# Where sequence 1's attention operands are made: inside layer 0's second MLP product, or behind it

## The chip, the cores and the metric

The kernel runs on one core of one Trainium2 chip. The metric is the device time of one execution in microseconds. The kernel before takes 1729.86 us (median of 3 runs, 1728.86 to 1730.07).

The core has a matrix engine (TensorE, "PE" in the profile, with its weight loads as "PEld"), a vector engine (VectorE, "DVE"), an activation engine (ScalarE, "ACT"), a general engine (GpSimd, "POOL"), and a sync engine (SyncE, "SP") that here only issues transfers. Each engine works off its own queue of instructions in a fixed order; an instruction that waits holds up everything behind it on its engine. Matmuls write to PSUM, eight banks of 128 x 512 floats. Everything else lies in SBUF.

## What is computed

Two sequences (512 tokens, 1024 features each, float32) go through two layers and a final norm:

```
x = x + fourier_mix(rms_norm(x, fourier_norm))            # layer 0
x = x + sq_relu_mlp(rms_norm(x, mlp_norm[0]))
x = x + gqa_attention(rms_norm(x, attn_norm), ...)        # layer 1
x = x + sq_relu_mlp(rms_norm(x, mlp_norm[1]))
y = rms_norm(x, final_norm)
```

with

```
rms_norm(x, g)   = x * rsqrt(mean(x*x, features) + 1e-6) * g
sq_relu_mlp(h)   = (max(h @ w_up, 0) ** 2) @ w_down       # 1024 -> 4096 -> 1024
gqa_attention(h) : qkv = h @ w_qkv (1024 -> 1536); q and k each rms_norm'ed per head of 128
                   and rotated; 8 query heads on 2 key/value heads; softmax; @ w_o
```

The change lies at the seam between layer 0's MLP and layer 1's attention.

## The kernel before

**Precision.** Every float32 matrix is split into a high half, which the matmul reads in its fast float32r form, and a low half, the rest. A product is then three matmuls: high by high, high by low, low by high (`mm3`, L76, and `product`, L827). A split is one ACT cast (L82, or with a gain per feature L86) and one DVE subtraction (L83, or L87).

**Layout.** The residual is kept with features on the partitions: `xs[q, m]` is a tile of 128 x 2 x 512 (feature blocks 2m and 2m+1, 512 tokens) for sequence q and m from 0 to 3. Most work tiles come from four pools: `u4` with 38 slots of 4 KB per partition (`slot()`, L61), `t2` with 8 of 2 KB (`tm()`, L64), `raw` with 5 for weights as they are loaded, and `w` with 4 for split weights (`own()`).

**The second MLP product of layer 0** (`second_product`, L1061, called at L1366) multiplies the 4096 hidden features of both sequences by `w_down`. It uses a block scheme of Winograd's kind: for each output pair m it keeps a shared sum `e[m]` and adds partial products to both sequences' `xs[q, m]`. Its steps are `Row` (two products of 12 matmuls) and `Sums` (five products of 12: t1, t3, t2, b22, t4), over four groups g of hidden features. The last group's four `Sums` (m = 0 to 3) close the product. For each, DVE forms sums of the raw weights (L1147 to L1149, L1155), splits them (L83), and adds the PSUM results to the residual (L1080). When all steps of m are done, `finish(m)` (L1241) adds `e[m]` to sequence 0 (L1244) and to sequence 1 (L1245), and calls `ready(m)`.

**What ready(m) does.** For both sequences it makes the two attention operands `hT[q][2m]`, `hT[q][2m+1]` (`make_h`, L177: ACT L86 and DVE L87, 128 x 512 each, with attn_norm as the gain), squares the two feature blocks on ACT (L157), adds the squares to `acc[q]` on POOL (L159; the first of a sequence needs no addition), and stores `xs[q, m]` to DRAM (`put_away`, L186, an SP transfer). The last of these closes the use of `xs[q, m]`, one `u4` slot.

**What follows.** PE starts attention with `begun` (L1482): the key/value columns (cg = 2) of sequence 0's four token tiles t, feature blocks 0 to 5, 18 matmuls each. Then comes `token_scale(0)` (L1349): `sums` (L161, eight tiny matmuls of `acc[0]` by ones, line L165) and a chain of small DVE and ACT instructions (L131 to L137) that gives the root r = rsqrt(mean square) of every token. Then, tile by tile, the last two feature blocks are added (6 matmuls), and the result is evacuated with the factor r: ACT L1507 for keys, ACT L86 and DVE L87 (128 x 256) for values, then the norm of the keys and the rotation (`norm_rope`, L1398, ending in the POOL addition L1423 into `kr[q]`). After tile 0's six matmuls stands `token_scale(1)`. Sequence 1's four tiles follow, 24 matmuls each. Before tile 2 of sequence 1, PE transposes sequence 0's keys (`transpose_k`, L1429, matmul line L1433), for which all four tiles of `kr[0]` must be there. In the same stretch DVE makes the rotation tables (L1378, 16 small instructions) and splits the next `w_qkv` weights (L83).

**What sets the order.** Inside `tc.manual_schedule(engines=...)` the named engines keep the order of the Python code. In the product's main loop (L1309) that is PE alone. For all other engines there, and for all engines from the end of the product up to the last stage's hand-ordered blocks, a planner in the framework makes one fixed order per engine before the run: it plays the program through and gives each engine the ready instruction that comes first in the code. A tile takes a slot of its pool when the planner places the first instruction that writes it. The functions that the change touches, and their callers:

Of the kernel before, what the change touches and what calls it, by code (L numbers as in the profile page):

```python
# [21 lines left out]
NSEQ = 2  # L22
NT = S // P
KC = D // P
# [16 lines left out]
def trunk_kernel(ctx, tc, x_in, xt_in, y_out, dcos, dsin, feat, rope, gfour, gcol, grow, gfin,  # L41
# [15 lines left out]
    def nm(s):  # L57
        n_[0] += 1
        return f"{s}_{n_[0]}"

    def slot(shape, dt):  # L61
        return act.tile(shape, dt, tag="u4", name=nm("u"))

    def tm(shape=(P, 512), dt=F32):  # L64
        return tmp.tile(list(shape), dt, tag="t2", name=nm("t"))
# [19 lines left out]
    def split_scaled(dst_hi, dst_lo, src, scale):  # L85
        nc.scalar.activation(dst_hi, src, AF.Copy, scale=scale)  # L86
        nc.vector.scalar_tensor_tensor(dst_lo, src, scale, f32(dst_hi), ALU.mult, ALU.subtract)  # L87
# [22 lines left out]
    def load_w(src, eng=nc.vector, parts=1, home=own):  # L110
        raw = load_raw(src)
        w = home()
        for i in range(parts):
            sl = slice(i * 1024 // parts, (i + 1) * 1024 // parts)
            split(w[0][:, sl], w[1][:, sl], raw[:, sl], eng)
        return w
# [5 lines left out]
    def rsqrt(out, ss, n, inv, room=None):  # L122
        for step in rsqrt_steps(out, ss, n, inv, room=room):
            step()
# [24 lines left out]
    def xt(q, fo):  # L149
        return xs[q, fo // 2][:, fo % 2]  # L150

    def square(q, fo, n=512):

        if fo == 0:
            acc[q] = tm()
        s = tm() if fo else acc[q]
        nc.scalar.activation(s[:, :n], xt(q, fo)[:, :n], AF.Square)  # L157
        if fo:
            nc.gpsimd.tensor_add(acc[q][:, :n], acc[q][:, :n], s[:, :n])  # L159

    def sums(q, n=NT):  # L161

        o = ps()
        for t in range(n):
            nc.tensor.matmul(o[:, 2 * t : 2 * t + 2], acc[q][:, t * P : (t + 1) * P], ones,  # L165
                             start=True, stop=True)
        return o[:, 0 : 2 * n : 2], o[:, 64:]
# [9 lines left out]
    def make_h(q, fo, g0):  # L177

        h = slot([P, 2, 512], F32R)
        split_scaled(h[:, 0], h[:, 1], xt(q, fo), gc[:, g0 + fo : g0 + fo + 1])  # L180
        return h
# [3 lines left out]
    def put_away(q, i):  # L185
        nc.sync.dma_start(park[q, i], xs[q, i])  # L186
# [1160 lines left out]
    hT, rs, wkv = [[], []], [], []  # L1347

    def token_scale(q):  # L1349
        r = sm.tile([P, NT], F32, tag="rs", name=nm("rs"), bufs=2)  # L1350
        ss, room = sums(q)
        rsqrt(r, ss, NT, 1.0 / D, room)
        rs.append(r)
# [2 lines left out]
        for _ in range(2):  # L1356
            wkv.append(load_w(w_qkv[2, len(wkv)], home=lent))

    def ready(m):
        for q in range(NSEQ):  # L1360
            for fo in range(2 * m, 2 * m + 2):
                hT[q].append(make_h(q, fo, KC))
                square(q, fo)
            put_away(q, m)

    second_product(0, blocks, rows, late, ready)  # L1366

    gb = tm((P, 4, HD))
    nc.sync.dma_start(gb, grow.to_broadcast([P, 4, HD]))
# [114 lines left out]
    for cg in (2, 0, 1):  # L1484
        ws = wkv if cg == 2 else [load_w(w_qkv[cg, u], home=own if u < 2 else lent) for u in range(4)]
        for q in range(NSEQ):
            if cg == 2:
                vt[q] = (slot([P, NT, 256], F32R), slot([P, NT, 256], F32R))
                kr[q] = slot([P, NT, 256], F32)
            else:  # L1490
                for i in range(2):
                    qr[q, 2 * cg + i] = slot([P, NT, 256], F32)
            for t in range(NT if (cg, q) != (1, 1) else 2):
                if (cg, q, t) in transposes:
                    transpose_k(transposes[cg, q, t])
                if (cg, q, t) == (1, 1, 1):
                    first = transpose_q(0, 0)
                if (cg, q) == (2, 0):
                    o = qkv(cg, q, t, ws, KC - 2, KC, begun[t])
                else:  # L1500
                    o = qkv(cg, q, t, ws)
                if (cg, q, t) == (2, 0, 0):
                    token_scale(1)
                r = rs[q][:, t : t + 1]
                if cg == 2:
                    raw = tm((P, 256))
                    nc.scalar.activation(raw, o[:, :256], AF.Copy, scale=r)  # L1507
                    split_scaled(vt[q][0][:, t], vt[q][1][:, t], o[:, 256:], r)
                    todo = norm_rope(raw, NKV, rt["k"], [t], [kr[q][:, t]])
                else:  # L1510
                    raw = tm()
                    nc.scalar.activation(raw, o, AF.Copy, scale=r)
                    todo = norm_rope(raw, 4, rt["q"], [t], [qr[q, 2 * cg + i][:, t] for i in range(2)])
                for _ in todo:
                    pass
# [325 lines left out]
```

## Time and profile before

| | |
|---|---|
| timed runs | 1728.86, 1729.86, 1730.07 us |
| the profiled execution's own time | 1727.7 us |
| its span, first to last instruction | 1725.9 us |
| PE busy in the span | 1693.2 us (98%) |
| DVE busy | 1244.9 us (72%) |
| ACT busy | 857.0 us (50%) |
| POOL busy | 332.6 us (19%) |
| PE's first attention matmul | 729.26 us |

The profile shows one execution. Times in it count from the start of its span. A row of the timeline reads: start, duration, engine, line of the kernel, operation, tiles written and read with their shapes, count, and in brackets how long the engine had been idle before it and what ended that. An engine with a "q" behind it is its queue, issuing a transfer. A row with a count above 1 is a run of equal instructions. A row of the windows view gives, for each stretch, each engine's busy time and instruction count, the mean granted TensorE clock (1.00 is full), and the mean share of the transfer engines; an instruction that laps into a stretch from before is counted in it.

### The profile page before, as it was taken

The numbers are of one execution on the slowest core, as the hardware profiler recorded it, in microseconds if no ns is written. First come the engines' busy times: TensorE is split into PE (matmuls) and PEld (weight loads), VectorE is DVE, ScalarE is ACT, GpSimd is POOL, SyncE is SP. The second block draws the span as 40 slices with busy tenths as digits, with TensorE's granted clock in tenths as the row PEclk, the third lists the DMA queues.
The fourth block names the chain that finished last, engine by engine and source line by source line (L and its number), as shares of the span: only waits on it lengthen the run. The fifth ranks groups of instructions, "written<-read, shape, count | busy, mean of one in ns | idle before, by whom it ended". The sixth has DMA issues, their size and how long they took to land. (4 is left out here: it accounts for less than half of the span.)

```text
span 1725.9 us, 21899 instructions
## 1 busy us (share of the span) xinstructions
PE 1693.2 (98%) x7847; PEld 1397.1 (81%) x7847; DVE 1244.9 (72%) x1836; ACT 857.0 (50%) x1508; POOL 332.6 (19%) x302
## 2 busy tenths in 40 slices
PE   9999999999999999999999999999999999999997
PEld 6987777888788888788877888788788888888886
DVE  8678777456887879975588834687755479687865
ACT  6665445446343434456687715554444554344334
POOL 1321442221000001322234303114322200000004
PEclk9999999999999999999999999999999999999999
DMA  9742555449554645520000213335543597455322
GB/s 321 188 153 86 183 183 172 170 172 358 208 195 135 211 147 179 186 88 27 25 25 1 98 49 122 105 123 182 180 150 141 210 305 253 150 211 190 120 74 98
DMA packets 103679, 266.33 MB, mean 154 GB/s; under 512 B 10177, under 2 KB 10177, under 8 KB 103570
## 3 DMA queue, kind: packets, MB, share of 16 engines
q1 hardware_dynamic: 87410, 232.95, 39.0%
q10 hardware_dynamic: 14112, 25.70, 4.0%
q0 software_dynamic: 2048, 6.29, 1.8%
q8 instruction: 61, 1.00, 0.2%
q14 instruction: 48, 0.39, 0.1%
HBM read 189.93 MB, written 73.92 MB: 153 GB/s over the span
## 5 line engine op out<-in xcount | busy, mean ns | idle before, releaser
L833 PE MATMUL ps<-u,w 128*128 128x512 f32 x4704 | 1079.2, 390 | 7.2 <-DVE w L83 5.1
L833 PEld LDWEIGHTS ps<-u,w 128*128 128x128 f32 x4704 | 882.9, 188 | 195.4 <-DVE w L83 7.5
L82 ACT CAST w<-raw 128x1024 fp32r<-128x1024 f32 (+1 forms) x226 | 220.7, 981 | 450.5 <-PE ps L833 260.6
L83 DVE TENSOR_TENSOR w<-raw,w 128x1024 fp32r<-128x1024 f32 (+1 forms) x226 | 263.5, 1168 | 73.9 <-ACT w L82 73.5
L159 POOL TENSOR_TENSOR t<-t,t 128x512 f32<-128x512 f32 (+1 forms) x56 | 80.1, 1434 | 733.1 <-ACT t L157 677.4
L83 DVE TENSOR_TENSOR u<-u,u 128x1024 fp32r<-128x1024 f32 x132 | 157.6, 1220 | 26.7 <-ACT u L82 25.9
L82 ACT CAST u<-u 128x1024 fp32r<-128x1024 f32 x132 | 132.4, 1044 | 71.1 <-PE ps L833 47.5
L77 PE MATMUL ps<-u,u 128*128 128x512 f32 (+2 forms) x388 | 150.1, 388 | 1.9 <-DVE u L496 1.4
L78 PE MATMUL ps<-u,u 128*128 128x512 f32 (+2 forms) x388 | 144.8, 373 | 1.1 <-DVE u L83 1.1
L1080 DVE TENSOR_TENSOR u<-ps,u 128x512 f32<-128x512 f32 x160 | 109.4, 686 | 50.3 <-PE ps L833 49.5
L79 PE MATMUL ps<-u,u 128*128 128x512 f32 (+2 forms) x388 | 144.5, 372 | 0.0
L833 PE MATMUL ps<-u,u 128*128 128x512 f32 x528 | 129.3, 396 | 8.5 <-DVE t L917 8.4
L833 PEld LDWEIGHTS ps<-u,u 128*128 128x128 f32 x528 | 99.0, 190 | 34.6 <-issue 8.0
L941 POOL TENSOR_TENSOR u<-u 128x512 f32<-128x512 f32 x28 | 36.5, 1304 | 422.2 <-ACT u L849 422.2
L83 DVE TENSOR_TENSOR u<-ps,u 128x512 fp32r<-128x512 f32 (+4 forms) x118 | 74.7, 651 | 18.1 <-ACT u L82 16.9
L77 PEld LDWEIGHTS ps<-u,u 128*128 128x128 f32 x388 | 73.5, 189 | 13.5 <-DVE u L496 1.6
L78 PEld LDWEIGHTS ps<-u,u 128*128 128x128 f32 x388 | 73.4, 189 | 13.2 <-DVE u L83 3.0
L79 PEld LDWEIGHTS ps<-u,u 128*128 128x128 f32 x388 | 73.1, 189 | 12.6
L82 ACT CAST u<-ps 128x512 fp32r<-128x512 f32 (+4 forms) x118 | 64.5, 561 | 28.9 <-PE ps L79 11.1
L816 DVE TENSOR_TENSOR u<-ps,u 128x512 f32<-128x512 f32 (+1 forms) x48 | 30.9, 645 | 64.7 <-PE ps L79 64.7
L906 DVE TENSOR_TENSOR t<-ps,u 128x512 f32<-128x512 f32 x30 | 20.7, 690 | 69.2 <-PE ps L833 64.0
L77 PE MATMUL ps<-u,w 128*128 128x512 f32 (+2 forms) x192 | 65.0, 339 | 0.0
(237 smaller groups left out, 1998.3 us busy)
## 6 DMA issues: line engine op xcount, KB each, us to landing
raw<-w_up SPq DMA_DIRECT2D x82, 512.0 KB, 4.6
u<-spill_t SPq DMA_DIRECT2D x60, 512.0 KB, 6.1
raw<-w_sum SPq DMA_DIRECT2D x56, 512.0 KB, 4.0
u<-spill_b SPq DMA_DIRECT2D x45, 512.0 KB, 5.4
spill_t<-u SPq DMA_DIRECT2D x87, 256.0 KB, 2.0
spill_b<-t ACTq DMA_DIRECT2D x60, 256.0 KB, 2.5
raw<-w_row SPq DMA_DIRECT2D x28, 512.0 KB, 4.4
park<-u SPq DMA_DIRECT2D x24, 512.0 KB, 3.0
```

Of the source, the lines that this page charges most:

```text
L77: nc.tensor.matmul(out, lh, rh, start=first, stop=False)
L78: nc.tensor.matmul(out, lh, rl, start=False, stop=False)
L79: nc.tensor.matmul(out, ll, rh, start=False, stop=last)
L82: nc.scalar.copy(dst_hi, src)
L83: eng.tensor_sub(dst_lo, src, f32(dst_hi))
L159: nc.gpsimd.tensor_add(acc[q][:, :n], acc[q][:, :n], s[:, :n])
L816: nc.vector.tensor_add(x[:, :n], o[:, :n], x[:, :n])
L833: nc.tensor.matmul(o, w[x][:, sl], h[k][y], start=first and k + i == 0, stop=k == n - 1 and i == 2, skip_group_check=not first)
L906: nc.vector.tensor_add(u2, ob, t[:, 0])
L941: eng.tensor_sub(t[:, 0], b12, b11)
L1080: nc.vector.tensor_add(x, o, x)
```

## The change

`ready(m)` now takes the sequence as a second argument, 0 if it isn't given. Inside the product it serves sequence 0 alone. Sequence 1's m = 0, 1 and 2 are called in one go behind the product, ahead of the rotation tables and of `begun` and `token_scale(0)` in the code. Sequence 1's m = 3 is called in the first pass of the key/value loop, behind sequence 0's tile 0, and `token_scale(1)` moves from there to behind sequence 1's own tile 0. No computation is added or removed.

```diff
-    def ready(m):
-        for q in range(NSEQ):
-            for fo in range(2 * m, 2 * m + 2):
-                hT[q].append(make_h(q, fo, KC))
-                square(q, fo)
-            put_away(q, m)
+    def ready(m, q=0):
+        for fo in range(2 * m, 2 * m + 2):
+            hT[q].append(make_h(q, fo, KC))
+            square(q, fo)
+        put_away(q, m)
 
     second_product(0, blocks, rows, late, ready)
+    for m in range(3):
+        ready(m, 1)
 
     gb = tm((P, 4, HD))
     nc.sync.dma_start(gb, grow.to_broadcast([P, 4, HD]))
...
                 else:
                     o = qkv(cg, q, t, ws)
                 if (cg, q, t) == (2, 0, 0):
+                    ready(3, 1)
+                if (cg, q, t) == (2, 1, 0):
                     token_scale(1)
                 r = rs[q][:, t : t + 1]
                 if cg == 2:
```

## The prediction

> **What bounds the kernel now.** I read the page first, then PE's waits, then windows around the longest wait, then each engine's timeline there.
>
> ```profile
> span 1725.9 us, 21899 instructions
> PE 1693.2 (98%) x7847; PEld 1397.1 (81%) x7847; DVE 1244.9 (72%) x1836; ACT 857.0 (50%) x1508; POOL 332.6 (19%) x302
> ```
>
> PE is busy for 98% of the span, so the change can only win back time that PE loses, and only where it waits for something that the change touches. PE's waits between 680 and 800 us, the seam:
>
> ```profile
> PE ps L833 <- DVE w L83: 3.9, 2, 2.3
> PE ps L1433 <- POOL u L1423: 0.7, 1, 0.7
> ```
>
> Two waits for split weights (3.9 us) and one for sequence 0's rotated keys (0.7 us). The windows show that the first two cost more than their idle time:
>
> ```profile
> 696.49:709.86 13.37, 13.37 (x60) 11.08 (x59) 13.36 (x16) 9.07 (x13) 6.09 (x4) 1.00 0.25 94
> 709.86:720.87 11.01, 7.12 (x23) 5.13 (x22) 11.01 (x12) 4.82 (x8) 4.18 (x4) 0.85 0.87 296
> 717.15:720.31 3.16, 3.15 (x7) 2.48 (x8) 3.16 (x4) 3.16 (x6) 2.87 (x2) 0.50 1.00 373
> ```
>
> The columns are busy time and count of PE, PEld, DVE, ACT, POOL, then granted clock and transfer share. In the first stretch 59 matmuls start (one lapped in) in 13.37 us: 0.2266 us each. In the second, 22 start; at that pace they need 4.99 us, not 11.01. So PE loses 6.0 us: 3.9 idle, 1.6 in the seven matmuls of the third row at clock 0.50 (3.16 - 7 x 0.2266), and 0.5 in the two restarts. DVE is busy without a break in both stretches: it is the bound there. PE's and DVE's timelines:
>
> ```profile
> 711.83 3.02 PE L833 MATMUL ps<-u,w 128*128 128x512 f32 x12 [1.57 <-DVE w L83]
> 717.16 12.27 PE L833 MATMUL ps<-u,w 128*128 128x512 f32 x46 [2.31 <-DVE w L83]
> 729.26 0.39 PE L77 MATMUL ps<-u,u 128*128 128x512 f32 x1
> ```
> ```profile
> 699.63 0.74 DVE L87 SCALAR_TENSOR_TENSOR u<-u,gc,u 128x512 fp32r<-128x512 f32 x1
> 700.29 1.78 DVE L1149 TENSOR_TENSOR raw<-raw,raw 128x512 f32<-128x512 f32 x1
> 701.99 3.49 DVE L87 SCALAR_TENSOR_TENSOR u<-u,gc,u 128x512 fp32r<-128x512 f32 x2
> 705.40 0.68 DVE L1080 TENSOR_TENSOR u<-ps,u 128x512 f32<-128x512 f32 x1
> 709.47 2.30 DVE L83 TENSOR_TENSOR w<-raw,w 128x1024 fp32r<-128x1024 f32 x1
> 711.70 0.68 DVE L1080 TENSOR_TENSOR u<-ps,u 128x512 f32<-128x512 f32 x1
> 714.03 0.68 DVE L1080 TENSOR_TENSOR u<-ps,u 128x512 f32<-128x512 f32 x1
> 715.29 0.68 DVE L1244 TENSOR_TENSOR u<-u,t 128x512 f32<-128x512 f32 x1
> 715.89 1.21 DVE L83 TENSOR_TENSOR w<-raw,w 128x1024 fp32r<-128x1024 f32 x1
> ```
>
> PE's first wait ends with the L83 of 709.47 (ends 711.77), its second with that of 715.89 (ends 717.10): the splits for the last Sums. Of the three operands made from 699.63 on, the code's order gives sequence 0 the first and sequence 1 the two at 701.99. They hold DVE from 701.99 to 705.40.
>
> **Does the planner really take them out of there?** ACT, POOL and DVE aren't ordered by hand here, and sequence 1's m = 1 is ready as early as before. The trace says that slots are handed out in the order of the code:
>
> ```profile
> 675.90 0.33 SPq L91 DMA_DIRECT2D raw<-w_qkv  x1
> ```
> ```profile
> 698.54 0.72 ACT L86 ACTIVATE u<-u,gc 128x512 fp32r<-128x512 f32 x1 [3.93 <-DVE u L1244]
> 701.44 0.61 ACT L157 ACTIVATE t<-u 128x512 f32<-128x512 f32 x1
> 701.96 1.04 ACT L82 CAST u<-raw 128x1024 fp32r<-128x1024 f32 x1
> 768.61 0.58 ACT L82 CAST u<-ps 128x512 fp32r<-128x512 f32 x1
> ```
> ```profile
> 765.48 0.44 PE L1433 MATMUL ps<-ident,u 128*128 128x128 f32 x2 [0.69 <-POOL u L1423]
> ```
> ```profile
> 768.49 0.74 POOL L1423 TENSOR_TENSOR u<-t,t 128x256 f32<-128x256 f32 x1 [3.06 <-DVE t L1421]
> ```
>
> The first w_qkv weight, sent for at 675.90, is cast at 701.96, although ACT sat idle for 3.93 us before 698.54: directly after ready(1), which stands ahead of it in the code. Sequence 0's transposed keys (the cast at 768.61, ready when the transposes of 765.48 ended) are cast directly behind the first L1423 of kr[1], whose slot was asked for earlier. So sequence 1's operands, now behind sequence 0's m = 3 in the code, can't get slots before it: they do move behind the product. By the same rule hT[1][6] and [7] come after kr[0], that is, after sequence 0's tile 0 has been rotated.
>
> **Step 1, the product's end.** Out of DVE's queue go 705.40 - 701.99 = 3.41 us. The first split then ends at 711.77 - 3.41 = 708.4; PE wants it at 711.83 - 1.57 = 710.26: no wait, 1.9 us in hand. The second ends at 717.10 - 3.41 = 713.7, after the L1080 now at 714.03 (then 710.62; its product ends at 710.26, so it can move that far). PE wants it one product later, at 710.26 + 12 x 0.2266 = 712.98: 0.7 us of wait remain, about 0.1 for its restart. Gain 6.0 - 0.8 = 5.2 us. Upper bound 6.0: with sequence 1's additions gone from POOL beside it, the L1149 of 1.78 us could lose up to 1 us, as an L87 takes 0.74 in one row above and 1.7 in another. Lower bound 3.6, if the half clock, which stands where the transfer share is 1.00, doesn't come from the waits.
>
> The Trainium skill bears on that last point ("TensorE: Matmul & The Clock Gate", Part 1: The HAM clock gate): half rate follows an idle window of about 3.4 us. Here it stands behind 2.31 us of idle, so by the page the 1.6 us wouldn't be the wait's and the gain would be 3.6 us. I take the trace's order of events, wait and then half clock.
>
> ACT's casts and SP's loads of the next weights only come earlier. Of sequence 1's four park transfers three move behind the product, ahead of the tables' input in SP's queue, and one behind tile 0; each holds SP for 0.33 us (as the issue at 675.90), which nobody waits for here.
>
> **Step 2, DVE behind the product.** The rows of before:
>
> ```profile
> 733.62 1.23 DVE L83 TENSOR_TENSOR w<-raw,w 128x1024 fp32r<-128x1024 f32 x1 [1.40 <-ACT w L82]
> 734.77 4.15 DVE L87 SCALAR_TENSOR_TENSOR u<-u,gc,u 128x512 fp32r<-128x512 f32 x3
> 738.84 2.30 DVE L83 TENSOR_TENSOR w<-raw,w 128x1024 fp32r<-128x1024 f32 x1
> 741.06 3.31 DVE L1378 SCALAR_TENSOR_TENSOR u<-raw,t 128x128 f32<-128x128 f32 x16
> 746.57 0.16 DVE L131 TENSOR_SCALAR s<-ps 128x4 f32<-128x4 f32 x1 [2.20 <-PE ps L165]
> ```
> ```profile
> L87 DVE SCALAR_TENSOR_TENSOR u<-u,gc,u x16: 734/744/1784, 668.0 to 737.1; 128x512 fp32r<-128x512 f32 x16
> L159 POOL TENSOR_TENSOR t<-t,t x56: 730/1292/2284, 66.5 to 1705.7; 128x512 f32<-128x512 f32 x49, 128x256 f32<-128x256 f32 x7
> 734.88 5.18 POOL L159 TENSOR_TENSOR t<-t,t 128x512 f32<-128x512 f32 x3 [10.32 <-ACT t L157]
> ```
>
> Sequence 0's root (L131) starts 746.57 - 729.26 = 17.3 us after the product; everything that DVE has ahead of it must fit in that. One L87 takes 0.74 us alone and up to 1.78 beside POOL's additions, which the moved squares bring along (five). I take the row of three with additions beside them, 4.15/3 = 1.38: six make 8.3 us. With the last L1080 and L1244 (1.4), sequence 0's own last L87 (0.7), two L83 (1.2 + 2.3, less 0.7, since only one of them needs to meet an addition, and perhaps not for its whole length) and L1378 (3.3): 16.5 us, and some 0.7 of waiting for ACT: 17.2. It just fits. Bounds: six at 0.74, 4.4 us, leave 4 us spare; six at 1.78, 10.7 us, make the root 2.5 us late. ACT needs 6 x (0.72 + 0.61) = 8 us for them, and POOL five of 1.7 (5.18/3), 8.6 us: both fit.
>
> **Step 3, sequence 1's first block.** In the times of before (everything shifts together):
>
> ```profile
> 762.99 0.70 ACT L1412 ACTIVATE t<-t,s 128x128 f32<-128x128 f32 x2 [1.02 <-DVE s L137]
> 745.59 0.95 PE L165 MATMUL ps<-ones,t 128*128 128x2 f32 x8
> 763.75 0.82 PE L1433 MATMUL ps<-ident,u 128*128 128x128 f32 x6
> 753.59 0.74 POOL L1423 TENSOR_TENSOR u<-t,t 128x256 f32<-128x256 f32 x1 [13.53 <-PE ps L79]
> 757.31 0.73 POOL L1423 TENSOR_TENSOR u<-t,t 128x256 f32<-128x256 f32 x1 [2.98 <-DVE t L1421]
> 764.70 0.72 POOL L1423 TENSOR_TENSOR u<-t,t 128x256 f32<-128x256 f32 x1 [2.99 <-DVE t L1421]
> ```
>
> Tile 0's L1423, now at 753.59, loses the second root from its way: seven small instructions of about 0.16 us (the L131 above), of which I take half to lie in its way, so an estimate of 0.6 us, and 753.0. Then ACT makes hT[1][6], its square, hT[1][7] (0.72 + 0.61 + 0.72, with tile 1's small work between: till 755.6) and DVE the last L87 (up to 1.78, till 757.4). PE comes to these blocks after 0.8 (sums) + 24 + 18 matmuls: 745.59 + 0.8 + 9.5 = 755.9, and needs the last of them at 757.1: 0.3 us of wait. POOL's last addition (1.7 each) ends near 758.2; the sums behind the block want it at 757.6: 0.6. Together +0.8; bounds 0, where the L87 and the additions take 0.74 and 1.29, and 2.5 more, where the root is late.
>
> **Step 4, the key transposes.** They wait 0.69 for tile 3's L1423. That comes 0.6 earlier by the removed root, 0.6 later by the same root in its new place, and later by what ACT's four inserted instructions (2.7 us) exceed its idle time in a tile (1.02 in the L1412 row, some 0.5 more at other waits, an estimate): 1.2. PE arrives 0.8 later: 0.4 more wait. Bounds: -0.7 (the wait is gone) to +2.
>
> **Sum.** -5.2 + 0.8 + 0.4 = -4.0 us. The profiled execution took 1727.7 us (1.8 beside its span), 2.2 under the median of the timed runs: 1723.7 there, 1725.9 as a median.
>
> **Rivals.**
> - *The second split stays late.* Without the two L87 the planner puts other ready work, say a split of w_qkv, in front of it: one L83 of 1.2 to 2.3 us brings its wait back to 2 or more, with the half clock. Only the first wait goes, 1.7 us with its restart: 1729.86 - 1.7 + 1.2 = 1729.4. For it: DVE has no idle time in 13.36 of 13.37 and 11.01 of 11.01 us. Against: 3.41 us go from directly ahead of it.
> - *Sequence 0's root comes late.* L87 and POOL additions in one batch take turns, all at 1.78: root, tile 0, hT[1][6..7] and tile 3 come 2.5 us later. PE pays once, at the first block: -4.0 + 2.5, 1728.4. The Trainium skill gives such a rule ("SBUF — State Buffer", Who interferes with whom): a VectorE instruction with two SBUF inputs and a GpSimd instruction that reads SBUF exclude each other, the later one blocked until the first ends. The 1784 against 734 ns above agrees with blocking.
> - *Slower: hT[1][6..7] come two tiles late.* They must follow kr[0]; if the planner also puts their ACT work behind tiles 1 and 2, L1423's spacing of 3.7 us makes PE's wait at the first block 0.8 + 7.4 = 8.2, with the half clock 9.8, less the transposes' 0.7: 1729.86 - 5.2 + 9.1 = 1733.8. It turns from gain to loss at about one tile. Against: they stand ahead of tile 0's evacuation in the code, so are taken first once slots are there.
> - *It doesn't do what it says.* The planner fills idle ACT and DVE time with sequence 1's work where it is now: 1729.9. Against: the slot order above.
>
> **How the numbers follow.** A measurement of this kernel tells about 0.2% (3.5 us) from no change, so faster means below 1726.4, slower above 1733.3. Chances: forecast 0.49 (0.42 under 1726.4, 0.07 above), second split 0.14 (same 0.12, faster 0.01, slower 0.01), root 0.14 (faster 0.02, same 0.11, slower 0.01), two tiles 0.15 (slower 0.12, same 0.03), no move 0.08 (same 0.06, slower 0.02). That makes 0.45, 0.39, 0.16. The forecast's own range goes from 1729.86 - 6.0 - 0.7 = 1723.2 to 1727.5 (half clock stays). The whole range reaches down to 1722.6 for the scatter of runs, and up to 1731.6, past all cases but two tiles late.
>
> **What would show it.** Right: no PE wait for L83 near 710 and no stretch at clock 0.50; PE's first L77 near 724; behind it six L87 in a row, some at 1.7; the root's L131 within a microsecond after its sums; small waits at the first L165 of acc[1] and at L1433. Wrong: L87 of sequence 1 still among the last Sums; a wait for L83 of 2 us; a wait for L87 of several us at sequence 1's first block.

## The result and the profile after

The changed kernel takes 1735.49 us (median of 6 runs, 1733.89 to 1737.65), the kernel before beside it 1727.81 us (6 runs, 1725.56 to 1730.07). The ratio is 1.0034, with a 95% interval of 1.0019 to 1.0048: slower by 0.0034 x 1728 = 5.9 us (3.3 to 8.3). (The two medians stand 7.7 us apart, inside that interval; the differences in this document go by the ratio.) The forecast was 4.0 us faster. The profiled execution took 1734.09 us, 1.8 of it beside the span.

The head of the page of the changed kernel, span and busy times:

```profile
span 1732.3 us, 21901 instructions
PE 1696.5 (98%) x7847; PEld 1398.9 (81%) x7847; DVE 1246.3 (72%) x1836; ACT 857.4 (49%) x1508; POOL 330.9 (19%) x302
```

The work is the same (PE's and DVE's counts did not move). PE's busy time is up by 3.3 us although it does the same 7847 matmuls: some of them ran slower. PE's waits in the seam, from 640 to 820 us:

```profile
PE ps L1434 <- POOL u L1424: 6.3, 2, 3.2
PE ps L833 <- DVE u L1080: 1.7, 2, 1.4
```

The two waits for the late splits (L83, 3.9 us) are gone. In their place PE waits 1.7 us for L1080 inside the product, and at sequence 0's key transposes, where it had waited 0.7 us, it now waits 6.3 (L1434 and L1424 are L1433 and L1423 of before, one line further down). PE's timeline at the transposes, and the window behind them:

```profile
761.54 0.38 PE L1434 MATMUL ps<-ident,u 128*128 128x128 f32 x2
765.14 0.55 PE L1434 MATMUL ps<-ident,u 128*128 128x128 f32 x3 [3.22 <-POOL u L1424]
768.78 0.90 PE L1434 MATMUL ps<-ident,u 128*128 128x128 f32 x3 [3.09 <-POOL u L1424]
```
```profile
769.00:773.60 4.60, 4.60 (x13) 3.73 (x13) 2.53 (x11) 3.34 (x15) 0.08 (x1) 0.50 0.00 0
```

PE is there two tiles ahead of the keys, and behind the second wait it runs at a granted clock of 0.50 for 4.6 us.

To see where the time went I set the matmuls of both traces side by side in their order and took the difference of their starts at three places. From the first matmul after 690 us to the product's end (the first L77, at 729.26 before and 726.99 after) the changed kernel gains 3.7 us; from there to 780 us it loses 8.2; in the rest it loses another 0.5. The first figure isn't simply 729.26 - 726.99 = 2.3, because the changed kernel's profiled execution was 1.4 us later from the first 100 us on, in code that is the same in both. So the seam costs 4.5 us in the profile. Both parts are what this document explains.

**Where the root went.** DVE's timeline behind the product, and PE's sums for sequence 0's root:

```profile
727.10 1.22 DVE L1245 TENSOR_TENSOR u<-u,t 128x1024 f32<-128x1024 f32 x1
729.02 1.23 DVE L83 TENSOR_TENSOR w<-raw,w 128x1024 fp32r<-128x1024 f32 x1 [0.69 <-ACT w L82]
730.16 0.68 DVE L1080 TENSOR_TENSOR u<-ps,u 128x512 f32<-128x512 f32 x1
730.88 0.69 DVE L1244 TENSOR_TENSOR u<-u,t 128x512 f32<-128x512 f32 x1
732.05 1.23 DVE L83 TENSOR_TENSOR w<-raw,w 128x1024 fp32r<-128x1024 f32 x1 [0.47 <-ACT w L82]
733.19 10.96 DVE L87 SCALAR_TENSOR_TENSOR u<-u,gc,u 128x512 fp32r<-128x512 f32 x7
744.08 5.49 DVE L1379 SCALAR_TENSOR_TENSOR u<-raw,t 128x128 f32<-128x128 f32 x16
749.49 1.41 DVE L87 SCALAR_TENSOR_TENSOR u<-u,gc,u 128x512 fp32r<-128x512 f32 x2
750.81 0.15 DVE L131 TENSOR_SCALAR s<-ps 128x4 f32<-128x4 f32 x1
```
```profile
743.31 0.95 PE L165 MATMUL ps<-ones,t 128*128 128x2 f32 x8
```

The sums end at 743.31 + 0.95 = 744.26 and the root (L131) starts at 750.81: 6.55 us late, with DVE busy throughout. In the kernel before it started 0.03 us after its sums. From 744.08 on DVE works on things that the root doesn't need: the tables and hT[1][6..7]. POOL's timeline beside it:

```profile
736.99 9.81 POOL L159 TENSOR_TENSOR t<-t,t 128x512 f32<-128x512 f32 x6 [0.19 <-POOL t L159]
768.00 0.72 POOL L1424 TENSOR_TENSOR u<-t,t 128x256 f32<-128x256 f32 x1 [2.92 <-DVE t L1422]
```

The tables take 5.49 us beside additions that end at 736.99 + 9.81 = 746.80; two additions lie beside them, and before, with none, the same sixteen instructions took 3.31. And the last rotated key tile comes at 768.00, 17.2 us after the root: tile follows tile at 3.7 us, so a late root is a late last tile.

### The profile page after: what moved, and what is told of

Its sections match the earlier page's. It is cut to its first block, busy times and chain, and to the rows that moved or that the text cites. A ratio compares the mean times of both kernels' runs of the same rounds, so it can differ in the third digit from the quotient of the medians.

```text
span 1732.3 us, 21901 instructions
## 1 busy us (share of the span) xinstructions
PE 1696.5 (98%) x7847; PEld 1398.9 (81%) x7847; DVE 1246.3 (72%) x1836; ACT 857.4 (49%) x1508; POOL 330.9 (19%) x302
## 3 DMA queue, kind: packets, MB, share of 16 engines
q1 hardware_dynamic: 87410, 232.95, 38.8%
## 5 line engine op out<-in xcount | busy, mean ns | idle before, releaser
L83 DVE TENSOR_TENSOR w<-raw,w 128x1024 fp32r<-128x1024 f32 (+1 forms) x226 | 260.1, 1153 | 75.1 <-ACT w L82 74.4
L83 DVE TENSOR_TENSOR u<-u,u 128x1024 fp32r<-128x1024 f32 x132 | 157.8, 1223 | 28.3 <-ACT u L82 27.7
L77 PE MATMUL ps<-u,u 128*128 128x512 f32 (+2 forms) x388 | 151.6, 392 | 1.9 <-DVE u L496 1.4
L1080 DVE TENSOR_TENSOR u<-ps,u 128x512 f32<-128x512 f32 x160 | 109.8, 688 | 51.0 <-PE ps L833 50.3
L833 PEld LDWEIGHTS ps<-u,u 128*128 128x128 f32 x528 | 99.1, 190 | 34.8 <-issue 8.4
L83 DVE TENSOR_TENSOR u<-ps,u 128x512 fp32r<-128x512 f32 (+4 forms) x118 | 74.7, 651 | 19.0 <-ACT u L82 17.9
L77 PEld LDWEIGHTS ps<-u,u 128*128 128x128 f32 x388 | 74.7, 192 | 13.6 <-DVE u L496 1.6
L78 PEld LDWEIGHTS ps<-u,u 128*128 128x128 f32 x388 | 74.6, 192 | 13.4 <-DVE u L83 3.0
L79 PEld LDWEIGHTS ps<-u,u 128*128 128x128 f32 x388 | 74.2, 191 | 13.0
L77 PE MATMUL ps<-u,w 128*128 128x512 f32 (+2 forms) x192 | 65.0, 338 | 0.0
```

What stands on the lines that cost most here:

```text
L77: nc.tensor.matmul(out, lh, rh, start=first, stop=False)
L78: nc.tensor.matmul(out, lh, rl, start=False, stop=False)
L79: nc.tensor.matmul(out, ll, rh, start=False, stop=last)
L83: eng.tensor_sub(dst_lo, src, f32(dst_hi))
L833: nc.tensor.matmul(o, w[x][:, sl], h[k][y], start=first and k + i == 0, stop=k == n - 1 and i == 2, skip_group_check=not first)
L1080: nc.vector.tensor_add(x, o, x)
```

## The experiments

**A** is the theory that came out of the comparison: sequence 0's root stands in DVE's queue behind work that POOL's additions stretch, its lateness goes through to the last key tile, and PE pays for it at the transposes. **B**, in the first four runs, puts the loss on the change's second part (the place of the last pair and of the second root); in the later ones on the added work as such.

The table has, for each kernel, the time against the kernel before of the same session; the gain in the product and the loss behind it (profile, as worked out above, in us); and how late the root starts after its sums end (from the rows of L165 and L131). Its last two columns are the two sides of PE's wait at the transposes: when the last tile of sequence 0's rotated keys is done (end of the fourth POOL addition of L1423, in us behind the product's end), and where in PE's order the last two transposes stand (matmuls behind the product's end; the kernel before starts the 167th at 36.2 us, with its wait of 0.7 us in it).

| kernel | ratio, 95% interval | product | root late | behind | last keys | last two transposes |
|---|---|---|---|---|---|---|
| before | 1 | 0 | 0.03 | 0 | 36.2 | 167, 168 |
| changed | 1.0034, 1.0019 to 1.0048 | -3.7 | 6.55 | +8.2 | 41.7 | 166, 167 |
| no additions | 0.9968, 0.9955 to 0.9980 | -3.9 | 0.03 | -0.5 | 35.4 | 166, 167 |
| root back | 1.0003, 0.9993 to 1.0013 | -3.6 | 5.60 | +4.1 | 40.9 | 170, 171 |
| squares behind | 0.9996, 0.9986 to 1.0005 | -4.9 | 3.86 | +4.8 | 39.4 | 167, 168 |
| operands behind | 1.0005, 0.9995 to 1.0014 | -5.7 | 4.84 | +6.7 | 40.6 | 167, 168 |
| root first | 0.9980, 0.9970 to 0.9990 | -4.0 | 0.03 | -0.4 | 38.9 | 181, 182 |
| m = 1 behind | 0.9986, 0.9976 to 0.9996 | -4.0 | 1.93 | +1.3 | 37.5 | 167, 168 |
| late root | 1.0024, 1.0015 to 1.0033 | -1.5 | 8.53 | +4.7 | 43.7 | 186, 187 |
| operands, root first | 0.9965, 0.9954 to 0.9977 | -5.7 | 0.73 | +0.1 | 40.4 | 185, 186 |
| late root, PE's order kept | 1.0061, 1.0044 to 1.0078 | +0.1 | 7.14 | +8.5 | 42.3 | 166, 167 |
| order only | 0.9997, 0.9987 to 1.0006 | -1.5 | 0.04 | -0.8 | 38.1 | 179, 180 |
| both roots | 0.9975, 0.9965 to 0.9985 | -5.6 | 0.18 | -0.6 | 38.8 | 181, 182 |

### The changed kernel without sequence 1's POOL additions (no additions)

```diff
             hT[q].append(make_h(q, fo, KC))
-            square(q, fo)
+            if q == 0 or fo == 0:
+                square(q, fo)
+            else:
+                nc.scalar.activation(tm(), xt(q, fo), AF.Square)
```

> The changed kernel with seven POOL additions left out: those of sequence 1's squares (L159), so sequence 1's root is made from its first feature block's squares alone. Theory A (DVE's queue): the changed kernel loses because sequence 0's root stands in DVE's queue behind nine L87 and the rotation tables, which POOL's additions beside them stretch from 733.2 to 750.8, so the root starts 6.5 us after its sums and PE waits 6.3 us at the key transposes and runs at half clock after that. Without the additions an L87 takes 0.74 us and is paced by ACT (1.15 us each), the tables 3.3 instead of 5.5 us: the root is then at most 2 us late, the transposes wait under 2 us, and the time falls by 5 to 8 us, to between 1 and 4 us under the kernel before. Theory B (the places of sequence 1's last pair and second root, in among sequence 0's tiles, cost the time): the additions don't matter, the wait at the transposes stays above 4 us and the time at 1734 or more.

Measured: 1726.01 against 1731.00 us, 0.9968: -5.5 us, where the changed kernel has +5.9. B falls, and the gain is somewhat more than A's 1 to 4 us. The kernel leaves out seven additions, so sequence 1's root is made from its first feature block alone. DVE's timeline:

```profile
736.05 3.77 DVE L87 SCALAR_TENSOR_TENSOR u<-u,gc,u 128x512 fp32r<-128x512 f32 x4
740.07 0.75 DVE L87 SCALAR_TENSOR_TENSOR u<-u,gc,u 128x512 fp32r<-128x512 f32 x1 [0.24 <-ACT u L86]
741.21 0.75 DVE L87 SCALAR_TENSOR_TENSOR u<-u,gc,u 128x512 fp32r<-128x512 f32 x1 [0.38 <-ACT u L86]
742.34 0.75 DVE L87 SCALAR_TENSOR_TENSOR u<-u,gc,u 128x512 fp32r<-128x512 f32 x1 [0.38 <-ACT u L86]
743.01 3.32 DVE L1382 SCALAR_TENSOR_TENSOR u<-raw,t 128x128 f32<-128x128 f32 x16
746.24 1.41 DVE L87 SCALAR_TENSOR_TENSOR u<-u,gc,u 128x512 fp32r<-128x512 f32 x2
747.63 0.16 DVE L131 TENSOR_SCALAR s<-ps 128x4 f32<-128x4 f32 x1
```

The order is that of the changed kernel. The seven operands and the tables take 743.01 + 3.32 - 736.05 = 10.3 us instead of 744.08 + 5.49 - 733.19 = 16.4, and the root meets its sums to 0.03 us. Six microseconds of DVE's time behind the product were the price of these seven additions, although PE waits for none of them in the changed kernel. Of PE's waits at the transposes 0.2 us are left.

### The first half of the change alone (root back)

```diff
-    for m in range(3):
+    for m in range(4):
         ready(m, 1)
...
                 if (cg, q, t) == (2, 0, 0):
-                    ready(3, 1)
-                if (cg, q, t) == (2, 1, 0):
                     token_scale(1)
```

> The changed kernel with the second half of the change undone: all four pairs of sequence 1 go behind the product (m = 3 too), and sequence 1's root returns to behind sequence 0's tile 0. Theory A (DVE's queue): nothing is taken out of DVE's queue ahead of sequence 0's root, so its start stays 5 to 8 us after the sums, PE's wait at the transposes stays at 5 us or more, and the time stays within 2 us of the changed kernel. Theory B (the places of the last pair and of the second root): the loss goes, the transposes wait about 1 us, and the time falls under that of the kernel before by the 3.7 us that the product's end gained.

Measured: 1.0003, no difference. Neither theory has it: A wanted the changed kernel's time, B a gain. The root is 5.6 us late here too (nine L87 in a row, then the tables), so its lateness doesn't hang on the second part; but it costs 4.1 us instead of 8.2. PE's waits:

```profile
PE ps L1434 <- POOL u L1424: 2.1, 1, 2.1
PE ps L1434 <- DVE s L131: 1.1, 1, 1.1
PE ps L165 <- POOL t L159: 1.0, 1, 1.0
```

The waits are single ones of 1.0 to 2.1 us, and behind none of them does the clock fall. The last two transposes stand four matmuls further back as well (170th matmul behind the product's end, 166th in the changed kernel). So the price of a late root isn't its length: it depends on where the transposes stand and on whether a wait ends in half clock.

### One half of the work each (squares behind, operands behind)

```diff
-                square(q, fo)
+                if q == 0:
+                    square(q, fo)
...
+    for fo in range(KC):
+        square(1, fo)
```

> The kernel before with only sequence 1's squares (ACT L157 and POOL L159) moved behind the product; its operands stay inside, its root stays where it was. Theory A (DVE's queue, and POOL stretching it): inside the product the L87 of sequence 1 at 701.99 take 0.74 instead of 1.7 us each and L1149 loses up to 1 us, 3 us in all, so PE's first wait (1.57) goes and the second (2.31) falls under 1; behind the product only three L87 and the tables meet the additions, so the root is at most 2 us late and the transposes wait at most 2.5 us: 1 to 4 us faster than before. Theory B (what was wrong is where sequence 1's last pair and root stand): as fast as before or faster, since these aren't moved. Against both: if the L87 themselves, not the additions, are what holds up the splits, both waits stay and the time is that of before.

Measured: 0.9996, no difference. The product gains 4.9, all of it is lost behind. Two rows of DVE and one of PE:

```profile
737.96 1.45 DVE L83 TENSOR_TENSOR w<-raw,w 128x1024 fp32r<-128x1024 f32 x1 [2.17 <-ACT w L82]
740.00 7.00 DVE L1381 SCALAR_TENSOR_TENSOR u<-raw,t 128x128 f32<-128x128 f32 x16 [0.59 <-DMA t<-grow]
```
```profile
765.22 0.44 PE L1436 MATMUL ps<-ident,u 128*128 128x128 f32 x2 [2.83 <-POOL u L1426]
```

Not one VectorE instruction was moved here, and the root is 3.86 us late. A split waits 2.17 us for an ACT cast that now stands behind the moved squares, and with four additions beside them the tables take 7.00 us, against 3.31. A had the root at most 2 us late and 1 to 4 us won: it counted three L87 and the tables as the only work that meets the additions, and left out the cast.

```diff
-                hT[q].append(make_h(q, fo, KC))
+                if q == 0:
+                    hT[q].append(make_h(q, fo, KC))
                 square(q, fo)
...
+    for fo in range(KC):
+        hT[1].append(make_h(1, fo, KC))
```

> The kernel before with only sequence 1's operands (ACT L86 and DVE L87) moved behind the product; squares and additions stay inside, and its root where it was. Theory A (DVE's queue): the two L87 at 701.99 leave the product, so both waits for the splits fall below 1 us in all, a gain of 3 to 5 us. Behind the product eight L87 stand ahead of the tables and the root, but with only three additions beside them: 7 to 9 us instead of 11, tables 3.3: the root 0 to 3 us late, the transposes' wait 1 to 4 us. Net between 4 us faster and no change. If instead the length of the batch doesn't matter without additions (all of the loss was contention), the transposes wait 0.7 as before and it is 3 to 5 us faster.

Measured: 1.0005, no difference. The product gains all that it had to give, 5.7 us, and has no wait left. Behind it the tables take 3.31 us, but eight more L87 stand ahead of the root, which is 4.84 us late, where A had 0 to 3; PE waits 5.0 us at the transposes, where A had 1 to 4. So neither half alone is harmless: each makes DVE's queue longer than it can be before the sums, the squares by holding up a cast and stretching the tables, the operands by standing there.

### The same work in another order (root first)

DVE's order behind the product is written out (manual_schedule for DVE, entered ahead of sequence 1's operands): six operands of sequence 1, sequence 0's root, the tables, then the rest.

```diff
+    behind = tc.manual_schedule(engines={ET.DVE})
+    behind.__enter__()
     for m in range(3):
         ready(m, 1)
-    gb = tm((P, 4, HD))
...
     token_scale(0)
+    gb = tm((P, 4, HD))
...
+    behind.__exit__(None, None, None)
```

> The changed kernel with one thing different: VectorE's order is written out behind the product, so that sequence 0's root stands ahead of the rotation tables and of hT[1][6..7]. The same work, in another order. A (the seam's end follows sequence 0's root, and the root waits in VectorE's queue): the product keeps its gain of 3.7 us, the root starts with its sums instead of 6.5 us after them, the tables and the pair behind it cost tile 0 1.5 to 3 us; against the kernel before -1 to -4 us. B (what costs is the added work itself, sequence 1's seven additions and four ScalarE instructions beside the tiles, wherever the root stands): as the changed kernel, +4 to +6 us.

Measured: 1727.00 against 1730.94 us, 0.998 (-3.5 us): A's. DVE's timeline, and PE's row of the last two transposes:

```profile
730.68 9.92 DVE L87 SCALAR_TENSOR_TENSOR u<-u,gc,u 128x512 fp32r<-128x512 f32 x7
742.72 0.16 DVE L131 TENSOR_SCALAR s<-ps 128x4 f32<-128x4 f32 x1 [2.12 <-PE ps L165]
744.04 3.61 DVE L1483 SCALAR_TENSOR_TENSOR u<-raw,t 128x128 f32<-128x128 f32 x16
747.58 1.40 DVE L87 SCALAR_TENSOR_TENSOR u<-u,gc,u 128x512 fp32r<-128x512 f32 x2
```
```profile
764.50 0.38 PE L1422 MATMUL ps<-ident,u 128*128 128x128 f32 x2
```

All of the moved work is there, additions too, and the seven operands still take 9.92 us. But now DVE waits 2.12 us for the root's sums instead of the root waiting 6.55 for DVE, and the tables, behind it, meet only the end of the additions. Between this kernel and the changed one lie some 9 us.

Two things changed, though, and not only the order of 18 DVE instructions. The root comes 6.5 us earlier behind the product (17.3 instead of 23.8 us), but the tables and a pair of operands now stand between it and tile 0's rotation, so the last keys come only 2.8 us earlier (38.9 instead of 41.7). And with DVE's order written out the planner also set the last two transposes 15 matmuls further back in PE's order, from the 166th and 167th to the 181st and 182nd, where PE has no wait for them. In this kernel PE starts its 166th matmul 35.5 us behind the product; at the changed kernel's place it would have waited some 3.3 us for keys that come at 38.9 (an estimate from these rows). No run has this DVE order with PE's order held, so how the 9 us are shared stays open.

### Only as much as fits (m = 1 behind)

The kernel before, with sequence 1's m = 1 pair alone moved behind the product; the other pairs stay.

```diff
+    def ready_most(m):
+        ready(m, 0)
+        if m != 1:
...
+            ready(m, 1)
...
+    second_product(0, blocks, rows, late, ready_most)
+    tail, hT[1] = hT[1][4:], hT[1][:2]
+    ready(1, 1)
+    hT[1] += tail
```

> The kernel before, with only sequence 1's m = 1 pair (two operands, two squares, two additions) moved behind the product; its other pairs stay where they were and the second root too. A: the two operands that stand ahead of the late splits are gone, gain at the product 4 to 5.5 us; behind it VectorE has two operands of some 1.4 us more against 2.2 us that the root of before waits for its sums, so the root is 0.6 us late: -3 to -5 us. B (the added work costs in its proportion, a quarter of the 8 us that the changed kernel loses behind the product): -2 to -3.5 us, with the root on time and the loss elsewhere.

Measured: 0.9986 (-2.4 us, 0.7 to 4.2). The product gains 4.0; the root is 1.93 us late, where A had 0.6, because the five L87 before it take 7.6 us (1.5 each). PE waits 2.0 us at the transposes, with no half clock. Less than A's range, and in B's; the root's lateness is A's mark, and it is there.

### A late root by itself (late root; late root, PE's order kept)

```diff
     begun = [qkv(2, 0, t, wkv, 0, KC - 2) for t in range(NT)]
-    token_scale(0)
+    table = rt["k"].rearrange("p a b c -> p (a b c)")[:, :512]
+    idle = tm((P, 512))
+    with tc.manual_schedule(engines={ET.DVE}):
+        for i in range(13):
+            nc.vector.scalar_tensor_tensor(idle, idle if i else table, 0.0, table, ALU.mult, ALU.add)
+        token_scale(0)
```

> The kernel before with thirteen idle VectorE instructions (the tables' own kind, 128x512, an estimate of 0.66 us each, 8.6 us in all, whose result nobody reads) between the tables and sequence 0's root; nothing else moves, no work of sequence 1 among it. The root comes some 6.4 us late, as in the changed kernel. A: PE waits 6 to 7 us more at the key transposes and then has a stretch at half clock of 1.5 to 2 us: +6 to +8.5 us, the product as before. B: a late root alone is hidden behind sequence 1's first blocks: +0 to +1.5 us.

Measured: 1.0024, +4.2 us: slower, so a late root isn't hidden, but less than A's 6 to 8.5. The root is 8.53 us late. The planner, which had these idle instructions before it, had spread the transposes over the 160th to 187th matmul behind the product's end; PE's waits there come to 1.6 + 1.9 us. In the next run PE's order is written out too, so that they stay together:

```diff
+    kept = tc.manual_schedule(engines={ET.PE})
+    kept.__enter__()
     begun = [qkv(2, 0, t, wkv, 0, KC - 2) for t in range(NT)]
...
-    with tc.manual_schedule(engines={ET.DVE}):
+    with tc.manual_schedule(engines={ET.DVE, ET.PE}):
...
     for cg in (2, 0, 1):
+        if cg == 0:
+            kept.__exit__(None, None, None)
```

> The kernel before with the same thirteen idle VectorE instructions ahead of sequence 0's root as in the run late root, and with TensorE's order written out as the code has it, so that the key transposes stay in front of the next matmuls instead of being spread among them, as the planner did there (160th to 187th matmul behind the product, against 160th to 168th in the kernel before and 160th to 167th in the changed one). The root comes some 7 us late again. A (a late root costs what PE's order can't hide, and the changed kernel's planner had not foreseen the lateness, so its transposes stood still): two or three waits of 2 to 3.5 us at the transposes, 6 to 7 us in all less 0.7, and 1.5 to 2 us of half clock: +6 to +8.5 us against the kernel before, where the run late root had +4.2. B (the price of a late root is the +4.2 us whatever PE's order): +3.5 to +5 us.

Measured: 1740.24 against 1730.71 us, 1.0061, +10.6 us (7.6 to 13.5): A's, somewhat above its range. PE's timeline at the transposes:

```profile
769.13 0.33 PE L1433 MATMUL ps<-ident,u 128*128 128x128 f32 x1 [0.24 <-POOL u L1423]
772.78 0.33 PE L1433 MATMUL ps<-ident,u 128*128 128x128 f32 x1 [3.32 <-POOL u L1423]
776.50 1.33 PE L1433 MATMUL ps<-ident,u 128*128 128x128 f32 x5 [3.39 <-DVE s L131]
```

These are the changed kernel's two waits (3.22 and 3.09), in a kernel in which no work of sequence 1 was moved. (The last is put down to an L131; POOL's last L1423 ended 0.06 us before the matmul started, so I read it as that.) With 7.14 us of lateness 8.5 are lost behind the product, as in the changed kernel with 6.55 and 8.2. So a late root alone is enough for the whole loss, with the transposes where they stand. (The kernel before has them at the 160th to 168th matmul, one matmul later, so the written PE order should cost little by itself; no run has it without the idle instructions.) The pair also suggests that the changed kernel's planner did not reckon with the lateness: its transposes stood at the 160th to 167th matmul, as close as before, and in the run before it spread them. What the planner reckoned with is shown by no run.

### Operands only, root first; its control; and the second root

The kernel of operands behind, with DVE's order written out as above: six operands, root, tables, two operands. The squares stay in the product.

```diff
+    behind = tc.manual_schedule(engines={ET.DVE})
+    behind.__enter__()
-    for fo in range(KC):
+    for fo in range(KC - 2):
         hT[1].append(make_h(1, fo, KC))
-    gb = tm((P, 4, HD))
...
     token_scale(0)
+    gb = tm((P, 4, HD))
...
+    for fo in range(KC - 2, KC):
+        hT[1].append(make_h(1, fo, KC))
+    behind.__exit__(None, None, None)
```

> The kernel before with sequence 1's operands behind the product (its squares and additions stay in it, as in the run operands behind, which gained 5.7 us at the product and lost 6.7 behind it), and with VectorE's order written out there: six operands, sequence 0's root, the tables, the last two operands. A: the root starts with its sums, so most of the product's 5.7 us stays: -3.5 to -5.7 us. B (operands behind the product cost as such): as operands behind, +0.5 to +1.5 us.

Measured: 1724.55 against 1730.94 us, 0.9965: -6.1 us (4.0 to 8.0), at the upper end of A's range and somewhat beyond. That beats both kernels. It is the lowest of the series, though its interval overlaps those of no additions, both roots and root first. The product's 5.7 us are kept; one wait of PE is left in the seam, as long as the one of the kernel before:

```profile
PE ps L1424 <- POOL u L1414: 0.7, 1, 0.7
```

But the keys tell that the early root is not what kept them. The fourth POOL addition and the transposes that wait, in operands behind and then in this kernel:

```profile
766.95 0.72 POOL L1426 TENSOR_TENSOR u<-t,t 128x256 f32<-128x256 f32 x1 [3.00 <-DVE t L1424]
764.01 0.66 PE L1436 MATMUL ps<-ident,u 128*128 128x128 f32 x4 [2.12 <-POOL u L1426]
767.73 0.69 PE L1436 MATMUL ps<-ident,u 128*128 128x128 f32 x2 [2.83 <-POOL u L1426]
```
```profile
766.10 0.74 POOL L1414 TENSOR_TENSOR u<-t,t 128x256 f32<-128x256 f32 x1 [2.99 <-DVE t L1412]
763.17 0.44 PE L1424 MATMUL ps<-ident,u 128*128 128x128 f32 x2 [0.69 <-POOL u L1414]
766.89 0.44 PE L1424 MATMUL ps<-ident,u 128*128 128x128 f32 x2
```

The product ends at 727.03 and at 726.47, so the last keys come 40.6 and 40.4 us behind it: nearly the same, since the tables and two operands stand between the root and tile 0's rotation now. What differs is PE's order. In operands behind the last two transposes are the 167th and 168th matmul, here the 185th and 186th, and PE's waits fall from 5.0 to 0.7 us. So of the 6.6 us between the two behind the product, most goes with the transposes' place, which the planner chose when DVE's order was written out.

Is it the written order itself that gains, with the transposes set back, even where nothing is moved? In the control the planner sets the last two 12 matmuls back (the 179th and 180th):

```diff
     begun = [qkv(2, 0, t, wkv, 0, KC - 2) for t in range(NT)]
+    behind = tc.manual_schedule(engines={ET.DVE})
+    behind.__enter__()
     token_scale(0)
+    gb = tm((P, 4, HD))
...
+    behind.__exit__(None, None, None)
```

> A control: the kernel before, with nothing moved out of the product, and only VectorE's order written out behind it so that sequence 0's root stands ahead of the rotation tables; the planner, which then knows the tables to come late, sets the last key transposes 18 matmuls further back, as it did in the runs root first and operands, root first. A (those two gained because the root met its sums, which PE gave 3.7 to 5.7 us earlier): here the sums come when they came, so nothing is gained but the 0.7 us wait at the transposes: -1 to +1.5 us. C (they gained from the written order itself, or from the transposes' place): -3 us or more.

Measured: 0.9997, no difference; A's, and C's 3 us are not there. That does not make the transposes' place worthless: here the last keys come 1.9 us later than in the kernel before (38.1 against 36.2) and PE, 12 matmuls later at them, has no wait. The written order, DVE's and with it PE's, gains only where the product has given something that can be kept. Last, the change's second part on top of the best kernel:

```diff
-                if (cg, q, t) == (2, 0, 0):
+                if (cg, q, t) == (2, 1, 0):
                     token_scale(1)
```

> The kernel of the run operands, root first (six operands of sequence 1 behind the product, sequence 0's root, the tables, the last two operands; squares left in the product), with the change's second part on top: sequence 1's root behind its first block. By A this second part is nearly free, as it only takes seven small VectorE instructions of 0.16 us out of tile 0's way: 0 to 1 us less than that run, -5.5 to -7.5 us against the kernel before. B (the second root's new place costs, as it then stands in tile 3's way ahead of the transposes): 1 to 3 us more than that run, -3 to -5 us.

Measured: 0.9975 (-4.3 us), inside B's range. But the two kernels' intervals overlap, so whether the second root's place is worth or costs 1 or 2 us stays open; the profile has no wait for it (PE waits once in the seam, 0.2 us for a split). The changed kernel's loss isn't there.

## Why the prediction was wrong

**The failed step is step 2, "it just fits".** It put the root at 17.3 us after the product, 2.5 late at worst. It came 750.81 - 726.99 = 23.8 us after. By the rows above, the 6.6 us over its 17.2 are:

- The last product work and the L83 ahead of the batch: the L87 start 733.19 - 726.99 = 6.2 us after the product, forecast 1.4 + 2.8 + 0.7 = 4.9. The sum left out sequence 1's own residual addition, the L1245 of 727.10, which takes until 728.32: 1.3 us. The two L83 are 0.5 us shorter than forecast and the waits for ACT 0.5 longer.
- Seven L87: 10.96 us, forecast 0.7 + 8.3 = 9.0: 1.9 us. At 1.57 each they lie between the two prices taken, nearer to the upper bound.
- The tables: 5.49, forecast 3.3: 2.1 us, with the overlap at their seams. The working took POOL's contention for the L87 alone and left the tables at their undisturbed row, though additions that last longer must run into them.
- hT[1][6..7]: 1.3 until the root starts, forecast none.

The last point is the **slot-order reading**. It was right for what leaves the product: none of sequence 1's work stayed there. But it also said that hT[1][6] and [7] come after kr[0], and they did not: ScalarE's pair ran at 740.90, in front of the root. Their squares came early too: POOL's batch has seven additions of sequence 1, where the working had five, and the two beside the tables are the last of them.

```profile
740.90 1.33 ACT L86 ACTIVATE u<-u,gc 128x512 fp32r<-128x512 f32 x2
```

Why the planner took them so early (they stand behind token_scale(0) in the code) no run was made for.

**Step 4's price was mis-sized** as a result: +0.4 us forecast, bounds -0.7 to +2. With two waits (6.3 instead of 0.7 us), the nine matmuls or so at half clock and the restarts it measured 8.2, everything behind the product taken together. The two rivals had half of it each. *Sequence 0's root comes late* had the mechanism and cut it off at 2.5 us, since it stretched the L87 only; and it let PE pay at sequence 1's first block, where the changed kernel has no wait at all. *Slower: two tiles late* had nearly the measured time, 1733.8 us against 1735.49, and PE is indeed two tiles ahead of the keys; but hT[1][6..7] weren't late, and the place is the transposes. The rule of the Trainium skill cited with the former ("SBUF — State Buffer", Who interferes with whom) is borne out by rows it was not applied to: the tables, with two SBUF inputs, take 3.31 us with no addition beside them, 5.49 with two and 7.00 with four.

**Step 1 was right in kind, wrong in two terms.** Forecast 5.2 us, measured 3.7. Both waits for L83 went. What is left are 0.25 and 1.45 us for L1080, and DVE's, ACT's and POOL's timelines say behind what:

```profile
718.91 0.68 DVE L1080 TENSOR_TENSOR u<-ps,u 128x512 f32<-128x512 f32 x1
719.51 3.96 DVE L83 TENSOR_TENSOR u<-raw,u 128x1024 fp32r<-128x1024 f32 x2
723.40 0.68 DVE L1080 TENSOR_TENSOR u<-ps,u 128x512 f32<-128x512 f32 x1
```
```profile
716.02 1.05 ACT L82 CAST w<-raw 128x1024 fp32r<-128x1024 f32 x1 [4.93 <-DMA raw<-w_qkv]
```
```profile
718.36 4.03 POOL L159 TENSOR_TENSOR t<-t,t 128x512 f32<-128x512 f32 x2 [12.43 <-ACT t L157]
```

The next w_qkv splits stand in front of the L1080 that frees PE's PSUM, and take 1.98 us each beside sequence 0's own additions. That is the rival *the second split stays late*, in a smaller form and at another instruction. ACT holds a cast that waits 4.93 us for its load in front of sequence 0's last operands; that this is what makes the splits late was not tried. The other term is the half clock. The trace's order of events, wait and then half clock, was taken for a rule; the runs show that the same wait does without it. The kernel before, then the runs order only and late root, each right behind a wait of 2.31 or 2.32 us for the same L83:

```profile
717.15:720.31 3.16, 3.15 (x7) 2.48 (x8) 3.16 (x4) 3.16 (x6) 2.87 (x2) 0.50 1.00 373
```
```profile
718.96:722.00 3.04, 3.04 (x13) 2.54 (x14) 3.04 (x4) 3.04 (x6) 2.77 (x2) 1.00 0.94 356
```
```profile
720.37:724.00 3.63, 3.63 (x16) 3.02 (x17) 3.63 (x4) 3.63 (x7) 3.28 (x3) 1.00 0.93 340
```

The clock is 0.50 in the first and 1.00 in the other two, at nearly the same transfer share: the whole "gain" of 1.5 us in the product that the table has for these two runs is that. So 1.6 of the 6.0 us were only sometimes there to be won. That the lower bound of 3.6 us stands so near the 3.7 measured is chance: the 3.7 has the half clock of this one profile of the kernel before in it, and against the run order only the changed kernel gains 2.2 in the product. With the 1.6 us left out, the profile's loss would be 4.5 + 1.6 = 6.1 us, and the timed one is 5.9; that this is the reason why they differ is argued, not shown.

**Step 3** forecast +0.8 us; PE has no wait there. Against the forecast of -4.0 us, the profile's +4.5 is thus 1.5 from step 1, -0.8 from step 3 and 7.8 from step 4: 8.5 us together.

The chances gave the outcome 0.16. What should have widened the range: the sum for DVE's queue came to 17.2 against 17.3, so each us not counted was a us of lateness at the root, and the bounds varied only one of its terms, the six operands.

## What to carry to other kernels

Before work is moved behind a stage, sum up the queue of the engine that the next critical small instruction stands on, and price every row in that queue with its new neighbours, not only the rows that move: here seven GpSimd additions, for none of which PE waited, cost VectorE 6 us. A gain at one wait is only kept if, at the next wait, the other input comes earlier by as much or the waiting engine comes to it later. Here PE had 0.7 us of wait at the transposes already, and the gain was kept where the keys came earlier (no additions) or where the transposes stood further back (root first; operands, root first). So when an order is written out, look at what the planner then does with the other engines: with the root behind the tables the same work lost 5.9 us and with the root ahead of them it won 3.5, but PE's order had changed as well.

## What the runs showed of the hardware

Whether a wait of TensorE is followed by half clock isn't set by its length alone. In these traces it followed the last wait at the transposes where that was 2.83 to 3.39 us (the changed kernel, squares behind, operands behind, late root with PE's order kept), and also where it was 1.95 (late root), but not where it was 2.03 or 2.14 (m = 1 behind, root back); in the product it followed 2.31 us in the kernel before and 2.28 in late root with PE's order kept, and not 2.32 in two other runs at the same instruction. The Trainium skill ("TensorE: Matmul & The Clock Gate", Part 1: The HAM clock gate) gives an idle window of about 3.4 us and calls it free-running; the free-running window agrees with a like wait that goes either way, but the 3.4 us does not agree with half clock behind waits as short as 1.95 and 2.28 us.

Single executions differ by several us in code that no edit touches: by the first matmul after 640 us the profiled runs of this series stand 0.1 to 5.0 us behind the kernel before's. A profile of one execution therefore has to be compared from a place just ahead of the change, as above, and not by its span.
